# Weight and bias of the norms between stages applied by channel, behind the transposes

## The chip, the cores and the metric

The kernel runs on one core of a Trainium2 chip. The metric is the device time of one execution in microseconds (us). The core has five engines that work side by side, each in the order of its own queue: TensorE (PE; its weight loads are shown as PEld), VectorE (DVE), ScalarE (ACT), GpSimd (POOL) and SyncE (SP, which here issues DMAs). Each core has one SBUF and eight PSUM banks, in which matmuls and transposes leave their results.

## The reference

The program is one inference step of a two-layer encoder for 512 prompt frames and 8 x 16 sample frames, 640 tokens of 1024 channels in float32. There are six sub-layers: a feed-forward block, a mixer (a diagonal state-space part beside stick-breaking attention), a feed-forward block, and in the second layer a feed-forward block, a Mamba-2 mixer and a feed-forward block. Each one is wrapped in a norm:

```python
def layer_norm(x, g, b):
    xf = x.astype(jnp.float32)
    mu = jnp.mean(xf, axis=-1, keepdims=True)
    var = jnp.mean(jnp.square(xf - mu), axis=-1, keepdims=True)
    return ((xf - mu) * lax.rsqrt(var + LN_EPS) * g + b).astype(x.dtype)

def swiglu(x, w_gate, w_up, w_down):
    return (jax.nn.silu(x @ w_gate) * (x @ w_up)) @ w_down
```

A sub-layer computes x <- layer_norm(ALPHA * x + sublayer(x)); the feed-forward blocks count half. The result y of a norm is used twice: as the input of the next sub-layer, and as the residual that is added to its output.

## The kernel before, in words

**Stages.** The six sub-layers run one after the other: ffn0, mix0, ffn1, ffn2, mix1, ffn3. Between them lie five boundaries, named B1 to B5 here, each with a norm. A sixth norm ends the program; the change leaves it as it is.

**Tiles.** The 640 tokens are five tiles of 128. The sum of residual and sub-layer is kept in `yacc` with tokens on partitions (128 x 5 x 1024). The products of a stage want channels on partitions: `xt["hi"]` and `xt["lo"]`, 8 blocks of 128 channels by 640 tokens. Each float32 operand is split into a high part in a rounded format (a CAST on ACT, L95) and the remainder (a subtraction on DVE, L96), and each product is three matmuls, high x high, low x high and high x low (`mm3`, L134).

**A boundary.** For each tile t, `tm_proj` does the last projection of the old stage: two halves of 512 channels, 12 matmuls each, and DVE adds each half to `yacc` (L209; at B2 and B5 other lines). Then `layer_norm` follows: bn_stats and bn_aggr on DVE (L168, L169), an add of epsilon (L170), the power -1/2 on POOL (L171), the product with the mean on DVE (`nm`, L174), the normalise pass on ACT, whole width (L175), then the multiplication by g and the addition of b along the row: the lower half's multiply on DVE (L177), the upper half's on POOL (L178), both adds on POOL (L180, L179). The fifth tile does this with two whole-width instructions on DVE (L182, L184). g and b lie in `g_bc`, broadcast to all partitions by two DMAs from POOL's queue (L158). Last come the transposes: four of 128 x 128 into each of two PSUM banks (L196), and each bank is split into `xt` by CAST and remainder.

**Order.** `layer_norm` only puts its transposes on the list `pend`. `run_pend` takes the oldest one out: after the third, fourth and fifth tile's projection for the first three tiles, so that tile t's transposes stand behind the projection of tile t + 2, and for the last two tiles between the products of the next stage. A product over tiles 0 and 1 (256 columns) needs only two tiles, and there are four such products; the pass over tiles 2 to 4 (384 columns) comes behind them and needs all. Projections, transposes and splits of a boundary share a ring of four PSUM banks; the next stage's products use the other four. Which bank a tile gets, the program's builder decides, and a bank is written again when its last reader is done. At B1, B3 and B4 the second tile's transposes take the two banks that the first tile's had; at B2 the first two tiles have banks of their own. The engines' queues are otherwise filled in the order in which a scheduler in the builder puts the instructions.

In the names below T0 to T4 are the transposes of the five tiles; `T1`, `T2` and `T4` with a number are SBUF buffers of the feed-forward stage that hold g and b.

Of the kernel before, what the change touches and what calls it, by code (L numbers as in the profile page):

```python
# [36 lines left out]
def kernel(ctx: ExitStack, tc: tile.TileContext, I, O, phases=PHASES):  # L37
# [36 lines left out]
    make_identity(nc, ident)  # L74
    mhalf = const.tile([128, 1], F32, name="mhalf")
# [80 lines left out]
    def load_gb(n, g_bc):  # L156
        for j in range(2):
            nc.gpsimd.dma_start(g_bc[j], bass.AP(tensor=I["ln_gb"].tensor, offset=I["ln_gb"].offset + (2 * n + j) * D,  # L158
                                                 ap=[[0, 128], [1, D]]))

    def layer_norm(t, g_bc, last):
# [10 lines left out]
        if t < NT - 1 and not last:  # L172
            nm = mv[:, 1:2]
            nc.vector.scalar_tensor_tensor(nm, mv[:, 0:1], -1.0, rs, op0=ALU.mult, op1=ALU.mult)  # L174
            nc.scalar.activation(y, y, AF.Identity, scale=rs, bias=nm)  # L175
            lo, hi = slice(0, 512), slice(512, 1024)
            nc.vector.tensor_tensor(y[:, lo], y[:, lo], g_bc[0][:, lo], op=ALU.mult)  # L177
            nc.gpsimd.tensor_tensor(y[:, hi], y[:, hi], g_bc[0][:, hi], op=ALU.mult)  # L178
            nc.gpsimd.tensor_tensor(y[:, lo], y[:, lo], g_bc[1][:, lo], op=ALU.add)  # L179
            nc.gpsimd.tensor_tensor(y[:, hi], y[:, hi], g_bc[1][:, hi], op=ALU.add)  # L180
        else:
            nc.vector.scalar_tensor_tensor(y, y, mv[:, 0:1], g_bc[0], op0=ALU.subtract, op1=ALU.mult)  # L182
            for c in [slice(0, 512), slice(512, 1024)] if last and t == NT - 1 else [slice(0, 1024)]:
                state["ln"] = nc.vector.scalar_tensor_tensor(y[:, c], y[:, c], rs, g_bc[1][:, c],  # L184
                                                             op0=ALU.mult, op1=ALU.add).ins
                if last:
                    nc.sync.dma_start(O["y"][t * 128:t * 128 + 128, c], y[:, c])
        if last:
            return
        xh, xl = xt["hi"], xt["lo"]  # L190

        def transposes():
            for j in range(2):
                pt = bank_b().rearrange("p (k c) -> p k c", c=128)
                for k in range(4):
                    nc.tensor.transpose(pt[:, k, :], y[:, (4 * j + k) * 128:(4 * j + k) * 128 + 128], ident)  # L196
                split(xh[:, 4 * j:4 * j + 4, t * 128:t * 128 + 128],
                      xl[:, 4 * j:4 * j + 4, t * 128:t * 128 + 128], pt)
# [13 lines left out]
    def ffn(i, ph, last, side=None):  # L212
# [4 lines left out]
        with ExitStack() as st:  # L217
# [46 lines left out]
            for h in range(2):  # L264
                o, L = HALVES[h]
                for f in fs:
                    pg, pu = (bank_a()[:, :L] for _ in range(2))
                    for p, u in ((pg, wg[f][0]), (pu, wg[f][1])):
                        mm3(p, [w_k(u, k) for k in range(KT)],
                            [(xh[:, k, o:o + L], xl[:, k, o:o + L]) for k in range(KT)])  # L270
                    s = row(f)[:, o:o + L]
# [3 lines left out]
                    run_pend()  # L275
# [1699 lines left out]
```

## Time and profile before

| | |
|---|---|
| median of 3 runs | 2573.09 us (2572.42 to 2573.87) |
| profiled execution | 2573.02 us |
| its span, first to last instruction | 2571.3 us |
| mean granted TensorE clock | 0.992 |
| the norm at B1: T0 to T4 | 441.18 to 466.87 us |
| PSUM banks per tile at a boundary | 2 |

A page of the profile gives each engine's busy time with its share of the span, the chain of work that ended last, and groups of equal instructions. A row of the timeline gives the start in us, the busy time in us (of all xN instructions of a row), the engine, the line and the operation with what it writes and reads, the shapes, and in brackets how long the engine had been idle and who ended that. A row of a group gives, behind the bar, the busy time in us and the mean of one in ns, then the idle time ahead of it. A row of the windows gives the stretch in us, its length, how long the engine was busy in it and with how many instructions, the granted TensorE clock, and the DMA's share and rate.

### The profile page before, as it was taken

Reading aid. Unit: us, or ns where it says so; the run is one execution under the profiler, and the core shown is the slowest. Engines: PE = TensorE matmul, PEld = TensorE weight load, DVE = VectorE, ACT = ScalarE, POOL = GpSimd, SP = SyncE. Lnnn points to the kernel's source line nnn. Section 1 sums busy time; section 2 is a strip of 40 time slices with the busy share of each in tenths; the row PEclk is TensorE's granted clock in tenths of the full one; section 3 lists DMA queues with packets and bytes.
Section 4 is the critical chain, followed back from the end, with each engine's and each line's share of the span. In section 5 each row is a group of like instructions: output and inputs, shape, how many; then the busy total and the mean of one; then the engine's idle time right before and its main releaser. Section 6 shows DMA issues by size and latency. Waiting matters only on the chain. (4 is left out here: it accounts for less than half of the span.)

```text
span 2571.3 us, 40672 instructions
## 1 busy us (share of the span) xinstructions
PE 2511.2 (98%) x15577; PEld 2297.1 (89%) x15577; DVE 2017.1 (78%) x3685; ACT 1225.1 (48%) x2329; POOL 287.3 (11%) x412
## 2 busy tenths in 40 slices
PE   8999999999899999999999999999999999999998
PEld 8999999878678999998999999889989878999997
DVE  7788877666768888887888887778686798876768
ACT  4443444336743555553455554566565443443332
POOL 0000002110030000003000002311111150000001
PEclk9999999999999999999999999999999999999999
DMA  5332334443311334443144434356564722443442
GB/s 183 107 97 86 107 115 153 150 159 101 96 53 55 107 96 110 119 126 105 53 111 114 116 106 132 114 184 193 159 203 141 238 72 80 161 150 110 143 138 95
DMA packets 174835, 317.44 MB, mean 123 GB/s; under 512 B 20480, under 2 KB 91776, under 8 KB 174128
## 3 DMA queue, kind: packets, MB, share of 16 engines
q1 hardware_dynamic: 164816, 293.83, 35.7%
q0 software_dynamic: 9824, 21.01, 4.0%
q8 instruction: 122, 2.00, 0.3%
q14 instruction: 73, 0.60, 0.1%
HBM read 259.56 MB, written 40.54 MB: 117 GB/s over the span
## 5 line engine op out<-in xcount | busy, mean ns | idle before, releaser
L96 DVE TENSOR_TENSOR w<-raw,w 128x512 fp32r<-128x512 f32 (+1 forms) x601 | 525.8, 899 | 84.7 <-ACT w L95 83.6
L95 ACT CAST w<-raw 128x512 fp32r<-128x512 f32 (+1 forms) x601 | 442.3, 776 | 289.7 <-PE bank L134 106.9
L356 PE MATMUL bank<-xhi,w 128*128 128x320 f32 x2432 | 540.0, 309 | 1.0 <-ACT mx L367 0.9
L134 PE MATMUL bank<-xhi,w 128*128 128x256 f32 (+2 forms) x2272 | 502.5, 313 | 14.5 <-ACT xhi L95 8.2
L134 PE MATMUL bank<-w,h 128*128 128x512 f32 x1872 | 435.1, 390 | 0.0
L356 PE MATMUL bank<-T,w 128*128 128x320 f32 x2736 | 426.3, 309 | 0.8 <-DVE s L393 0.4
L134 PEld LDWEIGHTS bank<-w,h 128*128 128x128 f32 x1872 | 349.2, 188 | 72.5 <-DVE h L96 1.0
L356 PEld LDWEIGHTS bank<-xhi,w 128*128 128x128 f32 x2432 | 407.4, 188 | 5.0 <-ACT mx L367 1.8
L356 PEld LDWEIGHTS bank<-T,w 128*128 128x128 f32 x2736 | 406.4, 188 | 2.8 <-DVE s L393 1.2
L134 PEld LDWEIGHTS bank<-xhi,w 128*128 128x128 f32 x2272 | 382.2, 190 | 26.1 <-ACT xhi L95 9.5
L356 PE MATMUL bank<-xlo,w 128*128 128x320 f32 x1216 | 375.1, 308 | 0.0
L134 PE MATMUL bank<-xlo,w 128*128 128x256 f32 (+2 forms) x1136 | 353.8, 312 | 5.8 <-DVE xlo L96 5.8
L356 PEld LDWEIGHTS bank<-xlo,w 128*128 128x128 f32 x1216 | 228.0, 188 | 0.3
L134 PEld LDWEIGHTS bank<-xlo,w 128*128 128x128 f32 x1136 | 215.9, 190 | 7.7 <-DVE xlo L96 7.0
L209 DVE SCALAR_TENSOR_TENSOR yacc<-bank,yacc 128x512 f32<-128x512 f32 x160 | 109.4, 687 | 77.8 <-PE bank L134 77.2
L367 ACT COPY mx<-bank 128x320 f32<-128x320 f32 x228 | 96.4, 423 | 142.2 <-PE bank L356 141.7
L96 DVE TENSOR_TENSOR w<-sw,w 128x1024 fp32r<-128x1024 f32 x76 | 93.0, 1224 | 52.9 <-ACT w L95 52.6
L95 ACT CAST w<-sw 128x1024 fp32r<-128x1024 f32 x76 | 79.8, 1051 | 99.0 <-DVE sw L335 97.9
L500 POOL DMA_DIRECT2D yacc<-ev x56 | 48.6, 904 | 651.2 <-ACT ev L499 591.2
L134 PE MATMUL bank<-w,og 128*128 128x512 f32 x432 | 104.9, 396 | 3.0 <-DVE og L1769 2.8
L134 PEld LDWEIGHTS bank<-w,og 128*128 128x128 f32 x432 | 79.6, 188 | 21.0 <-DVE og L1769 4.6
L395 ACT ACTIVATE s<-s 128x320 f32<-128x320 f32 x108 | 50.8, 471 | 84.0 <-DVE s L393 83.8
(428 smaller groups left out, 3467.0 us busy)
## 6 DMA issues: line engine op xcount, KB each, us to landing
raw<-in_w_gate_dram SPq DMA_DIRECT2D x88, 512.0 KB, 3.8
raw<-in_w_up_dram SPq DMA_DIRECT2D x88, 512.0 KB, 4.0
raw<-in_w_down_dram SPq DMA_DIRECT2D x88, 512.0 KB, 3.6
raw<-in_m_in_dram SPq DMA_DIRECT2D x52, 512.0 KB, 4.6
yacc<-ev POOLq DMA_DIRECT2D x56, 256.0 KB, 4.3
raw<-in_m_out_dram SPq DMA_DIRECT2D x24, 512.0 KB, 4.1
csb<-cs_d SPq DMA_DIRECT2D x20, 512.0 KB, 4.9
h<-in_ssd_h_dram SPq DMA_DIRECT2D x16, 512.0 KB, 6.1
```

Of the source, the lines that this page charges most:

```text
L95: nc.scalar.copy(hi, src)
L96: return nc.vector.tensor_tensor(lo, src, hi.bitcast(F32), op=ALU.subtract)
L134: state["pe"] = nc.tensor.matmul(ps, a, b, start=(k == 0), stop=(k == n - 1)).ins
L209: state["acc"] = nc.vector.scalar_tensor_tensor(ya, pb, scale, ya, op0=ALU.mult, op1=ALU.add).ins
L356: nc.tensor.matmul(ps, A[p][:, a, k * 128:k * 128 + 128], B[p][b][:, k, :], start=(first and n == 0), stop=(n == 11), skip_group_check=True)
L367: nc.scalar.copy(e[n], ps)
L395: state["silu"] = nc.scalar.activation(t, ps, AF.Silu).ins
L500: nc.gpsimd.dma_start(yacc[:, t, 512 * j:512 * j + 512], e, accum_op=ALU.add)
```

## The change

For the five norms between stages:

- Every tile gets `nm` (L187) and the normalise pass on ACT (L188). The multiply and add by row ahead of the transposes are gone, for the fifth tile too.
- The transposes read the normalised values. Behind the four transposes into a bank, ACT goes over the bank in four pieces of 128 x 128, with g as scale and b as bias by channel, which are partitions there (L200). Then come the CAST and the remainder, as before.
- The residual gets g and b on POOL behind that: four instructions of 128 x 512 a tile, two multiplies and two adds (L206). They overwrite what the transposes read, so they wait for them.
- g and b by channel lie in `gb_all`, a table of 128 x 96 that one DMA from SP's queue loads at the start, behind the loads of x.
- The broadcast g and b take other buffers (T2 and T4 in the feed-forward stage; at B5 four halves).
- The last two tiles' transposes move: T3 behind the first product of the next stage and T4 behind the third, where they stood behind the second and the fourth (in mix1 behind the first and the second).

```diff
@@ layer_norm
-        if t < NT - 1 and not last:
-            nm = mv[:, 1:2]
-            nc.vector.scalar_tensor_tensor(nm, mv[:, 0:1], -1.0, rs, op0=ALU.mult, op1=ALU.mult)
-            nc.scalar.activation(y, y, AF.Identity, scale=rs, bias=nm)
-            lo, hi = slice(0, 512), slice(512, 1024)
-            nc.vector.tensor_tensor(y[:, lo], y[:, lo], g_bc[0][:, lo], op=ALU.mult)
-            nc.gpsimd.tensor_tensor(y[:, hi], y[:, hi], g_bc[0][:, hi], op=ALU.mult)
-            nc.gpsimd.tensor_tensor(y[:, lo], y[:, lo], g_bc[1][:, lo], op=ALU.add)
-            nc.gpsimd.tensor_tensor(y[:, hi], y[:, hi], g_bc[1][:, hi], op=ALU.add)
-        else:
+        if last:
...
+        nm = mv[:, 1:2]
+        state["ln"] = nc.vector.scalar_tensor_tensor(nm, mv[:, 0:1], -1.0, rs, op0=ALU.mult, op1=ALU.mult).ins
+        nc.scalar.activation(y, y, AF.Identity, scale=rs, bias=nm)
         xh, xl = xt["hi"], xt["lo"]
+        gb_t = state["gb_t"]
 
         def transposes():
+
+            c = slice(t * 128, t * 128 + 128)
             for j in range(2):
                 pt = bank_b().rearrange("p (k c) -> p k c", c=128)
                 for k in range(4):
                     nc.tensor.transpose(pt[:, k, :], y[:, (4 * j + k) * 128:(4 * j + k) * 128 + 128], ident)
-                split(xh[:, 4 * j:4 * j + 4, t * 128:t * 128 + 128],
-                      xl[:, 4 * j:4 * j + 4, t * 128:t * 128 + 128], pt)
+                for k in range(4):
+                    nc.scalar.activation(pt[:, k, :], pt[:, k, :], AF.Identity, scale=gb_t[:, 0, 4 * j + k:4 * j + k + 1],
+                                         bias=gb_t[:, 1, 4 * j + k:4 * j + k + 1])
+                split(xh[:, 4 * j:4 * j + 4, c], xl[:, 4 * j:4 * j + 4, c], pt)
+            for op, g in ((ALU.mult, g_bc[0]), (ALU.add, g_bc[1])):
+                for j in range(2):
+                    yj = y[:, 512 * j:512 * j + 512]
+                    nc.gpsimd.tensor_tensor(yj, yj, g[j] if isinstance(g, list) else g[:, 512 * j:512 * j + 512], op=op)
@@ ffn
                         mm3(p, [w_k(u, k) for k in range(KT)],
                             [(xh[:, k, o:o + L], xl[:, k, o:o + L]) for k in range(KT)])
+                        if p is pg:
+                            run_pend()
...
-                    run_pend()
@@ mix0
                     u_tile(m, h)
-                    if m % 2:
+                    if m % 2 == 0:
                         run_pend()
@@ mix1
             xbc_half(0, 0, 0)
+            run_pend()
             xbc_half(0, 1, 0)
             dt_half(0)
+            run_pend()
             gate_half(0, 0, 0)
@@ the load of x
                 nc.sync.dma_start(yacc[:, t, :], I["x"][t * 128:t * 128 + 128, :])
+            nc.sync.dma_start(gb_all.rearrange("p n j k -> p (n j k)"), I["ln_t"])
```

Three places in the order of the instructions, all at B1 (B3 and B4 have the same ones). The first is POOL's queue, from the power of one tile on; `rs` is the power, T1 and T2 hold g and b. Before:

```order
L171 TENSOR_TENSOR rs_4338<-rs_4338,mhalf_80 128x1
L178 TENSOR_TENSOR yacc_84<-yacc_84,T1_4284 128x512
L180 TENSOR_TENSOR yacc_84<-yacc_84,T2_4285 128x512
L179 TENSOR_TENSOR yacc_84<-yacc_84,T2_4285 128x512
L171 TENSOR_TENSOR rs_4380<-rs_4380,mhalf_80 128x1
```

With the change (`rs_4416` is the third tile's, `rs_4480` the fourth's, `rs_4544` the fifth's; T2 holds g and T4 holds b):

```order
L178 TENSOR_TENSOR rs_4340<-rs_4340,mhalf_81 128x1
L178 TENSOR_TENSOR rs_4378<-rs_4378,mhalf_81 128x1
L206 TENSOR_TENSOR yacc_85<-yacc_85,T2_4286 128x512 x2
L206 TENSOR_TENSOR yacc_85<-yacc_85,T4_4287 128x512
L178 TENSOR_TENSOR rs_4416<-rs_4416,mhalf_81 128x1
L206 TENSOR_TENSOR yacc_85<-yacc_85,T4_4287 128x512
L206 TENSOR_TENSOR yacc_85<-yacc_85,T2_4286 128x512 x2
L206 TENSOR_TENSOR yacc_85<-yacc_85,T4_4287 128x512
L178 TENSOR_TENSOR rs_4480<-rs_4480,mhalf_81 128x1
```

Two powers now stand ahead of the first tile's residual, and the third tile's power stands behind three of its four pieces, the fourth tile's behind three of the second tile's. At B5 it is all four, and a power for the mixer's own norm (L1770) stands between.

The second place is ACT's queue at the first tile's banks. Before, the two casts follow the second normalise pass:

```order
L175 ACTIVATE yacc_84<-yacc_84,mv_4379,rs_4380 128x1024
L95 CAST xhi_82<-bank_4434 128x4x128
L95 CAST xhi_82<-bank_4441 128x4x128
L175 ACTIVATE yacc_84<-yacc_84,mv_4421,rs_4422 128x1024
L95 CAST xhi_82<-bank_4490 128x4x128
```

With the change:

```order
L188 ACTIVATE yacc_85<-yacc_85,mv_4377,rs_4378 128x1024
L200 ACTIVATE bank_4424<-bank_4424,gb_all_80 128x128 x2
L200 ACTIVATE bank_4435<-bank_4435,gb_all_80 128x128
L200 ACTIVATE bank_4424<-bank_4424,gb_all_80 128x128
L200 ACTIVATE bank_4435<-bank_4435,gb_all_80 128x128
L188 ACTIVATE yacc_85<-yacc_85,mv_4415,rs_4416 128x1024
L200 ACTIVATE bank_4424<-bank_4424,gb_all_80 128x128
L200 ACTIVATE bank_4435<-bank_4435,gb_all_80 128x128
L96 CAST xhi_83<-bank_4424 128x4x128
L200 ACTIVATE bank_4435<-bank_4435,gb_all_80 128x128
L96 CAST xhi_83<-bank_4435 128x4x128
```

The third tile's normalise pass, which takes `rs_4416` above, now stands between the fifth and the sixth of T0's eight scales, ahead of both of T0's casts.

The third place is PE at the second tile's transposes, with the engines that each row waits for. Before:

```order
L196 MATMUL bank_4490<-ident_75,yacc_84 128x128 [waits DVE_49,Pool_49]
L196 MATMUL bank_4490<-ident_75,yacc_84 128x128 x3
L196 MATMUL bank_4497<-ident_75,yacc_84 128x128 [waits DVE_49]
L196 MATMUL bank_4497<-ident_75,yacc_84 128x128 x3
L134 MATMUL bank_4504<-w_4258,h_3898 128x512 [waits DVE_49]
```

With the change:

```order
L198 MATMUL bank_4488<-ident_75,yacc_85 128x128 [waits DVE_49,Activation_49]
L198 MATMUL bank_4488<-ident_75,yacc_85 128x128 x3
L198 MATMUL bank_4499<-ident_75,yacc_85 128x128 [waits DVE_49]
L198 MATMUL bank_4499<-ident_75,yacc_85 128x128 x3
L135 MATMUL bank_4514<-w_4260,h_3900 128x512 [waits DVE_49]
```

The wait for POOL is gone and one for ACT has come. `bank_4499` is the PSUM bank that `bank_4424` was, so its wait for DVE is one for the remainder of the first tile's first half; `bank_4514`, the fifth tile's projection, is the bank that `bank_4435` was. Before, both banks of the second tile's transposes were those of the first tile's.

More of the change, by code (lines that the diff above doesn't have):

```diff
@@ L74 @@
     make_identity(nc, ident)
+    gb_all = const.tile([128, 6, 2, 8], F32, name="gb_all")
     mhalf = const.tile([128, 1], F32, name="mhalf")
@@ L156, in load_gb @@
     def load_gb(n, g_bc):
+        state["gb_t"] = gb_all[:, n]
         for j in range(2):
[L158 to L159 removed]
+            parts = g_bc[j] if isinstance(g_bc[j], list) else [g_bc[j]]
+            L = D // len(parts)
+            for k, part in enumerate(parts):
+                nc.gpsimd.dma_start(part, bass.AP(tensor=I["ln_gb"].tensor,
+                                                  offset=I["ln_gb"].offset + (2 * n + j) * D + k * L,
+                                                  ap=[[0, 128], [1, L]]))
     def layer_norm(t, g_bc, last):
@@ L523, in down @@
                     g_bc = [wk.tile([128, 2, 4, Q], F32, name=f"T{n}", bufs=1).rearrange("p a k c -> p (a k c)")[:, :D]
-                            for n in (1, 2)]
+                            for n in ((1, 2) if last else (2, 4))]
                     load_gb(norm, g_bc)
@@ L1814, in mixer1 @@
                 if c == 0:
-                    g_bc = [wk.tile([128, 2, 512], F32, name="h0", bufs=4).rearrange("p a b -> p (a b)")
-                            for _ in range(2)]
+                    g_bc = [[wk.tile([128, 512], F32, name=n, bufs=2) for _ in range(2)] for n in ("xd", "xe")]
                     load_gb(LN_OF[ph], g_bc)
```

10 lines of the change are left out of this document (3 added, 7 removed).

## The prediction

> **What bounds the kernel now.** I read the page's busy shares first, then its chain.
>
> ```profile
> PE 2511.2 (98%) x15577; PEld 2297.1 (89%) x15577; DVE 2017.1 (78%) x3685; ACT 1225.1 (48%) x2329; POOL 287.3 (11%) x412
> PE 14%; DVE 2%; DMA 0%; issue 0%; ACT 0%; POOLq 0%; DVEq 0%; ACTq 0%
> ```
>
> TensorE is busy 98% of the span and leads the chain, so the change is worth what it does to TensorE's gaps at the five boundaries, B1 to B5. ACT's 48% and POOL's 11% are averages over the whole program and say little about 35 us at a boundary. The gaps stand in the timeline of PE; first B1, from the first tile's transposes (T0) to the last (T4):
>
> ```profile
> 441.18 1.04 PE L196 MATMUL bank<-ident,yacc 128*128 128x128 f32 x8
> 447.54 1.03 PE L196 MATMUL bank<-ident,yacc 128*128 128x128 f32 x8
> 453.88 1.04 PE L196 MATMUL bank<-ident,yacc 128*128 128x128 f32 x8
> 454.67 0.48 PE L134 MATMUL bank<-xhi,w 128*128 128x256 f32 x2
> 460.28 1.09 PE L196 MATMUL bank<-ident,yacc 128*128 128x128 f32 x8
> 466.87 1.03 PE L196 MATMUL bank<-ident,yacc 128*128 128x128 f32 x8
> 468.14 1.14 PE L134 MATMUL bank<-xhi,w 128*128 128x384 f32 x5 [0.24 <-ACT xhi L95]
> 472.11 0.69 PE L134 MATMUL bank<-xlo,w 128*128 128x384 f32 x1 [2.83 <-DVE xlo L96]
> ```
>
> A block of transposes costs TensorE 0.79 (453.88 to 454.67), a tile's projection 447.54 - 441.18 - 0.79 = 5.57, and one product of the next stage over the first two tiles (460.28 - 454.67) / 2 = 2.8. Without a wait the pass over tiles 2 to 4, which needs T4's split, would begin 5 x 0.79 + 2 x 5.57 + 4 x 2.8 = 26.3 after T0. B1 loses 0.24 + 2.83 = 3.07. The gaps of B2 (first row), B3 (two), B4 (two) and B5 (the rest):
>
> ```profile
> 784.22 1.97 PE L134 MATMUL bank<-xhi,w 128*128 128x384 f32 x5 [4.73 <-ACT xhi L95]
> 1207.16 1.14 PE L134 MATMUL bank<-xhi,w 128*128 128x384 f32 x5 [0.24 <-ACT xhi L95]
> 1209.17 0.44 PE L134 MATMUL bank<-xlo,w 128*128 128x384 f32 x1 [0.87 <-DVE xlo L96]
> 1620.61 1.09 PE L196 MATMUL bank<-ident,yacc 128*128 128x128 f32 x8 [1.61 <-POOL yacc L179]
> 1626.17 1.07 PE L196 MATMUL bank<-ident,yacc 128*128 128x128 f32 x8 [1.64 <-DVE yacc L184]
> 2102.08 1.09 PE L196 MATMUL bank<-ident,yacc 128*128 128x128 f32 x8 [0.83 <-POOL yacc L179]
> 2113.78 0.98 PE L134 MATMUL bank<-w,og 128*128 128x512 f32 x3 [2.06 <-DVE og L1769]
> 2115.06 3.48 PE L134 MATMUL bank<-w,og 128*128 128x512 f32 x14 [0.31 <-DVE og L1769]
> 2135.32 1.14 PE L134 MATMUL bank<-xhi,w 128*128 128x384 f32 x5 [2.72 <-ACT xhi L95]
> 2138.54 0.69 PE L134 MATMUL bank<-xlo,w 128*128 128x384 f32 x1 [2.08 <-DVE xlo L96]
> ```
>
> B2 loses 4.73, B3 1.11, B4 3.25, B5 8.0. What follows a gap shows in windows of 4 us (instructions, then the granted clock):
>
> ```profile
> 472.00:476.00 4.00, 3.89 (x12) 0.50 1.03 409
> 784.00:788.00 4.00, 3.78 (x12) 0.50 0.00 0
> 788.00:792.00 4.00, 4.00 (x24) 0.95 0.00 0
> 1626.00:1630.00 4.00, 3.83 (x34) 1.00 0.29 77
> ```
>
> After 2.83 and 4.73 idle, 12 matmuls run where 24 do at 0.95: 2.0 lost, and 0.2 behind it, 2.2 in all. After 1.61 and 1.64 (B4) nothing is lost. So a gap's price jumps between 1.64 and 2.83. The Trainium skill (TensorE: Matmul & The Clock Gate, Part 1) puts that jump at an idle window of about 3.4 us. The trace differs, with half rate after 2.83. By the page the waits of about 4.5 below are slowed too and the sum is the same, but the short waits in mid-boundary could not be, and the contention rival below would come to 2606.
>
> **The change, part by part.** *Removed:* the multiply and add by channel ahead of the transposes. DVE's part (one half a tile, and all of the last tile) PE's projections hide; where it or POOL's was late, it is in the gaps above (B4's 1.61 and 1.64, B5's 0.83), and I count those gaps as gone. *The last two transposes* move ahead by one product each, 2.8, so that a product covers their split. *The new DMAs* (one table at the start, first used 440 us later; the broadcasts in other buffers, two halves each at B5) are hidden by that distance; uncovered they would cost one landing.
>
> *Added on POOL* is what decides. The residual's four pieces now wait until a tile has been transposed, and in POOL's order the power of the tile after next stands behind three of them (four at B5). POOL and ACT at B1 before:
>
> ```profile
> 441.97 1.81 POOL L178 TENSOR_TENSOR yacc<-yacc,T 128x512 f32<-128x512 f32 x1 [1.55 <-ACT yacc L175]
> 443.87 1.29 POOL L180 TENSOR_TENSOR yacc<-yacc,T 128x512 f32<-128x512 f32 x1
> 445.12 1.30 POOL L179 TENSOR_TENSOR yacc<-yacc,T 128x512 f32<-128x512 f32 x1
> 446.37 0.56 POOL L171 TENSOR_TENSOR rs<-rs,mhalf 128x1 f32<-128x1 f32 x1
> ```
>
> ```profile
> 441.82 1.08 ACT L95 CAST xhi<-bank 128x512 fp32r<-128x512 f32 x2
> 447.15 1.24 ACT L175 ACTIVATE yacc<-yacc,mv,rs 128x1024 f32<-128x1024 f32 x1 [4.26 <-DVE mv L174]
> 454.80 2.69 ACT L95 CAST w<-raw 128x512 fp32r<-128x512 f32 x5
> ```
>
> A piece is 1.30 (L178's 1.8 has a multiply of DVE beside it), power to ACT's normalise 446.37 to 447.15, 0.78, the first bank full 0.64 after T0. A cast is 0.54.
>
> *Added on ACT:* eight 128x128 instructions a tile with two pointers, in the bank. No row has this; the nearest:
>
> ```profile
> L1542 ACT ACTIVATE acc<-ext,cw 128x128 f32<-128x128 f32 x24 | 11.7, 488 | 0.0
> 1637.35 1.20 ACT L1542 ACTIVATE acc<-ext,cw 128x512 f32<-128x512 f32 x2
> 2091.79 0.97 ACT L1768 ACTIVATE og<-yb,chp 128x128 fp32r<-128x128 f32 x3
> L209 DVE SCALAR_TENSOR_TENSOR yacc<-bank,yacc 128x512 f32<-128x512 f32 x160 | 109.4, 687 | 77.8 <-PE bank L134 77.2
> L96 DVE TENSOR_TENSOR xlo<-bank,xhi 128x512 fp32r<-128x512 f32 x50 | 33.0, 664 | 3.4 <-ACT xhi L95 3.3
> L272 ACT ACT_TABLE_LOAD x3 | 3.8, 1283 | 0.1
> L754 ACT COPY g<-bank 128x256 f32<-128x256 f32 x4 | 1.5, 373 | 4.8 <-PE bank L134 4.6
> L1661 ACT COPY bk<-bank 128x128 f32<-128x128 f32 x20 | 5.3, 263 | 1.0 <-DVE cbm L1657 1.0
> ```
>
> L1542 has scale and bias by pointer, 0.49 by itself; L1768, one pointer, follows every 0.3 (three in 0.97, the last one whole). These are the bounds, since each of the new ones has two pointers, and L1661's 0.26, a copy without any, is too far off for more than a rival. I take 0.40: L1542's 0.49 less an overlap of 0.1 (its two forms together took 1.20, the longer one 0.825 by its own group's mean).
>
> B1, us after T0's start. POOL: 0.65 + 3 x 1.30 = 4.55, power, third tile's normalise on ACT 5.33 to 6.57. Two queues stand behind this one wait. On DVE, behind the small product that takes the power, stand the next projection's accumulation, a BN_STATS and T0's remainders xlo; the first two (L209's 0.69, and about as much) are done by 6.9. On ACT, behind the normalise, stand the last scales and the casts of T0: the first cast ends at 7.9, the second at 8.85, and DVE's remainders (0.65) at 8.55 and 9.5. Who waits for those is PE, for the banks: in the built program T1's second bank is T0's first, so T1's second half, due at 6.76, waits until 8.55 (1.8), and the fifth tile's projection, due at 8.95 and using T0's second bank, until 9.5 (0.55). Round again: T1's second bank is full at 9.0, two pieces to 11.6, fourth normalise 12.4 to 13.6, T1's casts 15.0 and 16.5, T2's second half waits 0.15. Mid-boundary: 2.5.
>
> From there ACT has no gap but one: two weight casts to 17.5, T2's eight to 20.7, cast 21.25, the fifth normalise (POOL's four pieces of T2 from 15.65, power) 21.65 to 22.9, cast 23.45, a weight cast 24.0, T3's eight 27.2, two casts 28.3, three weight casts 29.9, three of T4 31.1, three copies at about 0.33 32.1, two more 32.9, T4's first cast 33.45. TensorE is there at 26.3 + 2.5 = 28.8 and waits 4.65. Loss 7.15 against 3.07: **+4.1**; half rate follows in both.
>
> B2: T0 and T1 have banks of their own, so T1 does not wait. T1's pieces run from 7.0, the fourth power at 11.2, normalise 12.0 to 13.2, T1's first cast 14.5; the next stage's first product, due at 13.5, waits 1.0 for it and some 0.3 in its middle for the second. What held T4's cast before is this:
>
> ```profile
> 783.07 0.62 ACT L95 CAST w<-raw 128x512 fp32r<-128x512 f32 x1 [3.35 <-DMA raw<-in_w_up_dram]
> ```
>
> A weight cast ahead of it waited for a landing; in the new order that cast stands behind T4's. ACT's chain is late instead: the walk of B1 with a table load (1.28), a silu and a cast of h, each about a copy's length, for the three copies puts T4's first cast at 33.5, where TensorE is at 27.6: loss 7.2 against 4.73, **+2.5**. B3, banks as B1, the table loaded already: cast at 33.25, loss 2.5 + 4.45 = 6.95 against 1.11, and a half-rate stretch that was not there, 5.8 + 2.2 = **+8.0**. B4, banks as B1, one more weight cast ahead of T4 and one less ahead of T3: cast at 33.4, loss 2.5 + 4.6 = 7.1 against 3.25, and 2.2, **+6.1**. B5: T0 comes at 2101.25, 0.83 sooner. Four pieces, a power for og and the norm's power end at 2108.2, T0's remainders at 2110.9 and 2112.5; a product that takes T0's first bank waits for the first, 1.7. The waits for og are over by then. The next stage's first product loses 0.5, T4's first cast ends at 2137.9 where TensorE is at 2131.7: 1.7 + 0.5 + 6.2 = 8.4 against 8.0, **+0.4**; both end in half rate.
>
> Sum 4.1 + 2.5 + 8.0 + 6.1 + 0.4 = 21.1. Against the profiled execution (2573.0: span 2571.3 and 1.7 around it; the median of the runs is 2573.1) that is **2594**.
>
> Bounds: 26 of the scales lie on the walk, at 0.30 each 2.6 less a boundary (-13, 2581), at 0.49 2.3 more (+12). POOL's first piece at 1.8 as L178: 0.5 a turn, two turns, +5. The waits of 1.8 and 0.55 may fall on the dear side of the clock's jump: +2.2 at three boundaries, +6.6. All three high: 2617.
>
> **Rivals.** *The gaps go (faster).* If banks or POOL's order did not bind and ACT kept up, the 20.2 of gaps and three half-rate stretches (6.6) could go: 2546 at best, half of it 2560. For it: no transpose waits for a POOL product any more, and T4 gains 2.8. Against: ACT alone, from T2's scales on, has 4 us more work than TensorE's 26.3 leaves. It decides if T4's first cast comes under 27 us after T0, which needs scales below 0.2. Chance 0.06.
>
> *Nothing measurable.* Scales at 0.26 as the plain copy L1661 and no half rate at B3 and B4: 21 - 26 x 5 x 0.14 - 4.4, about -1.5, 2571.5, within the 0.2% (5 us) that a measurement of this kernel can tell. Chance 0.06.
>
> *Contention (slower still).* POOL now works 20 pieces a boundary rather than 12, beside DVE's weight splits, and both lengthen: pieces of 1.8 throughout, 5 on each walk, +2.5 a boundary, and half rate already at T1: 21 + 12 + 7, 2613. Decides from where T1's wait passes 2.8. Chance 0.14.
>
> **Numbers.** Forecast 0.74. Slower by over 0.2%: 0.74 + 0.14 = 0.88; within: 0.06; faster: 0.06. Range 2581 to 2614: the bounds of the scales below, the contention case above.
>
> **What would show it.** Right: at B1, B3, B4 the second half of T1's transposes waits about 1.8 for DVE's xlo, POOL's powers (now L178) start behind three pieces, ACT is without a gap for 15 us up to T4's casts, and PEclk falls to 0.5 at all five boundaries. Wrong: no wait at T1, scales of a mean under 0.35 with a cadence of 0.2, or T4's cast ahead of the fourth product's end.

## The result, and the profile after

The changed kernel takes 2606.13 us (median of 4 runs, 2604.38 to 2607.74), the kernel before, run beside it, 2572.76 us (4 runs, 2570.48 to 2573.87). The ratio is 1.0126, interval [1.0112, 1.014]: 33 us slower.

From the profiled execution (span 2606.0 us), the page's busy shares and the head of its chain:

```profile
PE 2520.6 (97%) x15577; PEld 2303.5 (88%) x15577; DVE 2017.5 (77%) x3660; ACT 1299.7 (50%) x2534; POOL 327.0 (13%) x454
PE 78%; DVE 9%; ACT 6%; issue 2%; DMA 2%; POOL 2%; SPq 0%; POOLq 0%; DVEq 0%; ACTq 0%
```

TensorE runs the same 15577 matmuls. It is busy 9.4 us longer than before (2520.6 against 2511.2), at a mean granted clock of 0.989 instead of 0.992, and idle 85.4 instead of 60.1 (each span less the busy time), 25.3 more. The chain now has POOL in it with 2% of the span; that of before covers only a sixth of its span, so the two are not compared share by share. Where TensorE idles, its timeline shows. B1 from T0 on (first seven rows), B2 (one row), B3 (three), B4 (two), B5 (two):

```profile
442.35 1.04 PE L198 MATMUL bank<-ident,yacc 128*128 128x128 f32 x8
449.40 0.63 PE L198 MATMUL bank<-ident,yacc 128*128 128x128 f32 x4 [0.56 <-DVE yacc L217]
451.89 0.66 PE L198 MATMUL bank<-ident,yacc 128*128 128x128 f32 x4 [1.86 <-DVE xlo L97]
452.84 5.75 PE L135 MATMUL bank<-w,h 128*128 128x512 f32 x24 [0.29 <-DVE xlo L97]
460.19 0.66 PE L198 MATMUL bank<-ident,yacc 128*128 128x128 f32 x4 [1.16 <-DVE xlo L97]
469.76 1.04 PE L198 MATMUL bank<-ident,yacc 128*128 128x128 f32 x8
478.84 1.65 PE L135 MATMUL bank<-xhi,w 128*128 128x384 f32 x4 [5.30 <-ACT xhi L96]
773.51 0.50 PE L135 MATMUL bank<-xhi,w 128*128 128x256 f32 x2 [2.79 <-ACT xhi L96]
1197.50 0.66 PE L198 MATMUL bank<-ident,yacc 128*128 128x128 f32 x4 [1.86 <-DVE xlo L97]
1198.44 7.35 PE L135 MATMUL bank<-w,h 128*128 128x512 f32 x24 [0.29 <-DVE xlo L97]
1226.29 1.97 PE L135 MATMUL bank<-xhi,w 128*128 128x384 f32 x5 [6.14 <-ACT xhi L96]
1631.89 1.06 PE L198 MATMUL bank<-ident,yacc 128*128 128x128 f32 x4 [1.87 <-DVE xlo L97]
1659.84 1.65 PE L135 MATMUL bank<-xhi,w 128*128 128x384 f32 x4 [4.87 <-ACT xhi L96]
2143.78 0.36 PE L1767 MATMUL bank<-ones,ext 128*128 128x2 f32 x2 [2.05 <-DVE xlo L97]
2172.06 1.97 PE L135 MATMUL bank<-xhi,w 128*128 128x384 f32 x5 [6.89 <-ACT xhi L96]
```

Two kinds of waits make up most of it: T1's second half for a bank (1.86, 1.86, 1.87), and the pass over tiles 2 to 4 for T4's cast (5.30, 6.14, 4.87, 6.89; B2's, not shown, 3.40). At B2 the first product waits for T1's cast (2.79), at B5 a product for the bank of T0 (2.05). The same matmul in both traces, followed through the program, gives what each boundary adds: B1 +5.2, B2 +3.5, B3 +11.9, B4 +10.7, B5 +2.0, together 33.3. The stages between them give or take at most 2.4 each, 0.3 in all, and the way up to B1 adds 1.2.

What feeds those waits is POOL's order at B1, here in POOL's timeline of the changed kernel, with the mean-by-power operation in DVE's timeline behind it:

```profile
443.08 3.79 POOL L206 TENSOR_TENSOR yacc<-yacc,T 128x512 f32<-128x512 f32 x3 [3.50 <-issue]
446.83 0.55 POOL L178 TENSOR_TENSOR rs<-rs,mhalf 128x1 f32<-128x1 f32 x1
447.35 1.29 POOL L206 TENSOR_TENSOR yacc<-yacc,T 128x512 f32<-128x512 f32 x1
465.59 0.55 POOL L178 TENSOR_TENSOR rs<-rs,mhalf 128x1 f32<-128x1 f32 x1
466.11 10.91 POOL L206 TENSOR_TENSOR yacc<-yacc,T 128x512 f32<-128x512 f32 x8
```

```profile
447.42 1.24 DVE L187 SCALAR_TENSOR_TENSOR mv<-mv,rs 128x1 f32<-128x1 f32 x1 [3.01 <-POOL rs L178]
455.71 1.24 DVE L187 SCALAR_TENSOR_TENSOR mv<-mv,rs 128x1 f32<-128x1 f32 x1 [1.17 <-POOL rs L178]
466.18 1.23 DVE L187 SCALAR_TENSOR_TENSOR mv<-mv,rs 128x1 f32<-128x1 f32 x1 [1.39 <-POOL rs L178]
474.22 4.15 DVE L97 TENSOR_TENSOR w<-raw,w 128x512 fp32r<-128x512 f32 x3
```

The power stands behind three residual pieces, as forecast. New is the row after it. A product of two 128 x 1 columns takes 1.24 us, and it ends at 448.66, when POOL's running piece ends (447.35 + 1.29 = 448.64). The weight splits too are long beside POOL's eight pieces: of the three in 4.15 the first two took 1.69 and 1.75, and the third, behind POOL's last piece (466.11 + 10.91 = 477.02), 0.88. Not every one is held: a split at 469.80 took 0.68 beside the same row of pieces.

The Trainium skill (GPSIMD Engine Reference, Specifications) says that POOL shares its SBUF interfaces with DVE and that DVE instructions with two SBUF inputs contend for them. Both held operations read two tensors from SBUF, so the trace agrees in these rows; the runs below test it by the operands.

The hold on the splits is not new. In the kernel before, two of them took 2.92 at B1 beside POOL's pieces at 454.97 and 456.86:

```profile
456.14 2.92 DVE L96 TENSOR_TENSOR w<-raw,w 128x512 fp32r<-128x512 f32 x2
```

ACT at B1, the fifth tile's normalise pass and one bank pair of scales in the timeline, and the scales' group:

```profile
461.67 2.91 ACT L200 ACTIVATE bank<-bank,gb_all 128x128 f32<-128x128 f32 x8
467.45 1.25 ACT L188 ACTIVATE yacc<-yacc,mv,rs 128x1024 f32<-128x1024 f32 x1 [2.36 <-DVE mv L187]
```

```profile
L200 ACT ACTIVATE bank<-bank,gb_all 128x128 f32<-128x128 f32 x200 | 76.5, 454 | 8.3 <-PE bank L198 7.8
```

ACT idles 2.36 ahead of the fifth normalise, so the chain there is led by POOL's turn and not by ACT's work.

### The profile page after: what moved, and what is told of

It reads as the page before. It is cut to its first block, busy times and chain, and to the rows that moved or that the text cites. A ratio compares the mean times of both kernels' runs of the same rounds, so it can differ in the third digit from the quotient of the medians.

```text
span 2606.0 us, 40900 instructions
## 1 busy us (share of the span) xinstructions
PE 2520.6 (97%) x15577; PEld 2303.5 (88%) x15577; DVE 2017.5 (77%) x3660; ACT 1299.7 (50%) x2534; POOL 327.0 (13%) x454
## 4 chain that ended last, share of the span: by engine, by line
PE 78%; DVE 9%; ACT 6%; issue 2%; DMA 2%; POOL 2%; SPq 0%; POOLq 0%; DVEq 0%; ACTq 0%
PE bank L135 34%; PE bank L365 30%; PE bank L497 6%; DVE w L97 2%; PE bank L1030 2%; POOL yacc L206 2%; ACT w L96 1%; ACT bank L200 1%; ACT yacc L188 1%; DVE mv L187 1%; PE bank L869 1%; ACT xhi L96 1%; ACT es L84 1%; PE bank L1737 1%; PE bank L1713 0%
## 5 line engine op out<-in xcount | busy, mean ns | idle before, releaser
L97 DVE TENSOR_TENSOR w<-raw,w 128x512 fp32r<-128x512 f32 (+1 forms) x601 | 532.0, 909 | 82.9 <-ACT w L96 81.6
```

Source lines behind the costliest of these rows:

```text
L97: return nc.vector.tensor_tensor(lo, src, hi.bitcast(F32), op=ALU.subtract)
```

## The experiments

The theory from these traces: the residual on POOL is the price, by the power's place behind the pieces and by the hold on DVE. Rivals: the banks that T1 shares with T0; ACT's scales; the new places of the last transposes.

| run | median us | ratio to before | interval |
|---|---|---|---|
| the change | 2606.13 | 1.0126 | 1.0112 to 1.014 |
| no residual | 2562.89 | 0.996 | 0.9945 to 0.9975 |
| powers first | 2607.31 | 1.0129 | 1.0109 to 1.0149 |
| mean-by-power with pointer | 2601.48 | 1.0116 | 1.01 to 1.0132 |
| new places alone | 2558.52 | 0.9947 | 0.9934 to 0.996 |
| residual on DVE | 2567.09 | 0.9983 | 0.9973 to 0.9993 |
| no scales | 2582.82 | 1.0042 | 1.0027 to 1.0057 |
| one-input pieces | 2599.84 | 1.0112 | 1.0093 to 1.0131 |
| powers first, one-input pieces | 2578.04 | 1.0022 | 1.0009 to 1.0036 |
| two tiles on the new way | 2579.01 | 1.0031 | 1.0019 to 1.0043 |
| one tile on the new way | 2563.45 | 0.9964 | 0.9949 to 0.9978 |
| places, bias add on DVE | 2559.59 | 0.9953 | 0.9938 to 0.9967 |
| places, weight and bias on DVE | 2548.28 | 0.991 | 0.9895 to 0.9925 |

**The residual left out.** The four POOL pieces a tile are gone; the next stage's residual lacks weight and bias.

```diff
-            for op, g in ((ALU.mult, g_bc[0]), (ALU.add, g_bc[1])):
-                for j in range(2):
-                    yj = y[:, 512 * j:512 * j + 512]
-                    nc.gpsimd.tensor_tensor(yj, yj, ..., op=op)
```

> The residual's multiply and add on POOL are left out, so the residual of the next stage lacks weight and bias; everything else is as in the change. Theory: as with the powers first, 2558 to 2570, since the pieces cost through their place and through what they hold up on DVE; a difference to the powers-first kernel of more than 4 us would be what POOL's work beside DVE's weight splits costs. Rival 1 (ACT's scales): 2590 or more.

2562.89 us, 43 below the changed kernel. At B1 one wait is left in PE's timeline:

```profile
470.40 1.14 PE L135 MATMUL bank<-xhi,w 128*128 128x384 f32 x5 [2.53 <-ACT xhi L96]
```

The pass waits 2.74, 2.79, 2.38 and 1.81 at the other boundaries. T1's bank is shared as before and costs nothing. So the residual carries more than the whole loss. With it gone, T4's cast behind ACT's scales still makes PE wait about 2.5 a boundary.

**Powers first.** The pieces are the same, but all five powers of a boundary stand ahead of them on POOL.

```diff
-            for op, g in ((ALU.mult, g_bc[0]), (ALU.add, g_bc[1])):
...
+            owed.append(residual)
+            if t >= 2:
+                with tc.issue_after(state["pow"]):
+                    while owed:
+                        owed.pop(0)()
```

> All five powers of a boundary stand ahead of every residual piece in POOL's queue; ACT's and PE's orders and the banks stay those of the change. Theory (the power behind three pieces, and DVE's small product held by the piece that follows the power, pace the boundary): the time from power to normalise falls from 1.86 to 0.8 us, the second half of T1's transposes no longer waits for xlo, T4's first cast comes 27 to 29 us after T0 instead of 36.5, and the time is 2560 to 2570, below before. Rival 1 (the eight scales a tile on ACT pace it): T4's cast stays later than 33 us after T0 and the time is 2590 or more. Rival 2 (the PSUM bank that T1 shares with T0): T1's wait of 1.9 us stays, 2595 or more.

2607.31 us: no gain at all, though the mid-boundary waits are gone, T1's on the shared bank among them. The time is that of the two rivals, but neither explains it: T1 does not wait, and the pass over tiles 2 to 4 begins 30 to 32 after T0 at B1 to B4. The loss has moved. Counted as above, B4 adds 17.8 here instead of 10.7; the other boundaries add less than in the changed kernel (B1 4.3, B3 5.5), and the stages behind B2 and B3 add 2.3 and 4.3, by what is open. POOL, DVE and PE at B4 (one row of each timeline), and the group of the weight splits:

```profile
1637.40 24.71 POOL L208 TENSOR_TENSOR yacc<-yacc,T 128x512 f32<-128x512 f32 x20
```

```profile
1644.99 17.68 DVE L97 TENSOR_TENSOR w<-raw,w 128x512 fp32r<-128x512 f32 x1
```

```profile
1666.18 0.69 PE L135 MATMUL bank<-xlo,w 128*128 128x384 f32 x1 [15.07 <-DVE xlo L97]
```

```profile
L97 DVE TENSOR_TENSOR w<-raw,w 128x512 fp32r<-128x512 f32 x384 | 289.8, 784 | 27.0 <-ACT w L96 26.7
```

With 20 pieces back to back, one split took 17.68 and ended at 1662.67, 0.56 behind POOL's last piece (1637.40 + 24.71 = 1662.11); three more followed it and were through at 1664.72. The remainder queued behind them on DVE keeps TensorE idle for 15.07. My expectation left that hold out. The bank rival falls here: shared bank, early power, no wait.

**The mean-by-power product with a pointer.** One operand (the power) is given as a per-partition scalar, so that only one tensor is read.

```diff
-nc.vector.scalar_tensor_tensor(nm, mv[:, 0:1], -1.0, rs, op0=ALU.mult, op1=ALU.mult)
+nc.vector.tensor_scalar(nm, mv[:, 0:1], rs, -1.0, op0=ALU.mult, op1=ALU.mult)
```

> The small product of mean and power on DVE takes the power as a pointer scalar instead of as a second tensor operand; all orders are those of the change. Theory (DVE's instruction with two tensor operands in SBUF is held until POOL's running piece ends): it takes 0.16 us instead of 1.24, each of three normalise passes a boundary comes 1.08 sooner, T4's first cast about 2 to 3 us sooner at each of five boundaries: 2592 to 2598. Rival (a pointer operand is held as well, or the 1.24 is off the path): unchanged, 2604 to 2608.

All 25 of them with their minimum, median and maximum in ns:

```profile
L187 DVE TENSOR_SCALAR mv<-mv,rs x25: 212/214/216, 434.3 to 2152.2; 128x1 f32<-128x1 f32 x25
```

In the changed kernel the same line ranges from 159 to 1242. This form is never held. But 2601.48 us lies between my two forecasts, only 4.7 below the changed kernel by the medians, and the two intervals overlap. At B1 T4's cast still keeps PE waiting 5.23: the fifth normalise comes 23.5 after T0 instead of 25.1, TensorE comes earlier too, and the fifth tile's statistics on DVE stand behind weight splits of 1.75, 1.81 and 1.18. That the hold ends with the pointer form is shown; that this is worth much by itself is not.

**The new places alone.** The norm of the kernel before, with T3 and T4 behind the first and third product.

```diff
+                        if p is pg:
+                            run_pend()
...
-                    run_pend()
```

> The norm of before; only the last two transposes stand behind the first and third product, as in the change. Theory (the place by itself is worth little, since the late stalls come from POOL and ACT): T4 is asked for 2.8 us sooner and so waits more for DVE's last multiply-add at B1 to B3, the pass behind it less: within 6 us of before, 2567 to 2579. Rival (the place carries part of the loss): 2580 or more.

2558.52 us, 14 faster than before and more than I expected. What is left at B1 in PE's timeline is POOL's last add ahead of T3:

```profile
457.84 1.09 PE L196 MATMUL bank<-ident,yacc 128*128 128x128 f32 x8 [2.60 <-POOL yacc L179]
```

So the new places gain 14 in the norm of before, and the changed kernel is 48 slower than they alone are. Whether the same 14 is still in the changed kernel is not shown.

**The residual on DVE.** Same place in the program, same pieces, other engine.

```diff
-                    nc.gpsimd.tensor_tensor(yj, yj, ..., op=op)
+                    nc.vector.tensor_tensor(yj, yj, ..., op=op)
```

> The changed kernel with one word changed: the four 512-wide pieces of the residual (weight, bias) stand on VectorE at the same place in the program, instead of POOL. VectorE gets 4 x about 0.69 us = 2.8 us a tile, 13.8 us a boundary. Theory (POOL's two-SBUF-tensor pieces hold VectorE's own two-SBUF-tensor operations and the powers behind them): the powers start at once, the mean-by-power operation takes 0.16 again, the w splits take 0.69 each again; what is left is the 2562.9 us of the kernel without a residual plus what 2.8 us of VectorE work a tile delays of the splits: 2565 to 2590. Rival (the work itself is the price, wherever it runs, because VectorE's evictions and splits are the bound at a boundary): 2600 or more.

2567.09 us, 39 below the changed kernel, with 2.8 us a tile more on DVE. All mean-by-power products take 159 to 162 ns, and the group of the weight splits stands at 692 ns a piece, against 736 in the changed kernel:

```profile
L187 DVE SCALAR_TENSOR_TENSOR mv<-mv,rs x25: 159/159/162, 430.9 to 2118.2; 128x1 f32<-128x1 f32 x25
L97 DVE TENSOR_TENSOR w<-raw,w 128x512 fp32r<-128x512 f32 x384 | 254.5, 692 | 41.7 <-ACT w L96 36.3 <-DMA raw<-in_m_v_dram 4.8
```

The work is not the price; its engine is. An engine that was 77% busy took it for 4 us over the kernel without a residual, from one at 13%.

**No scales.** The changed kernel without ACT's scale and bias in the bank; the next stage's input lacks both.

```diff
-                for k in range(4):
-                    nc.scalar.activation(pt[:, k, :], pt[:, k, :], AF.Identity, scale=..., bias=...)
```

> The changed kernel without ScalarE's scale and bias in the bank (left out: the weight and bias of the next stage's input); the residual stays on POOL. If the costs add up (placement -14, scales in the bank about +4, residual on POOL +43 to the 2572 of before), 2598 to 2606. If ScalarE's chain of scales behind the last transposes is a price of its own that the residual only hides, 2580 to 2595.

2582.82 us, the second forecast of the two. With the residual on POOL, the scales cost 23. Without them PE's waits for T4's cast are gone (none named xhi stands in its table of waits), but three others came, two rows of that table:

```profile
PE bank L135 <- ACT hf L279: 13.2, 3, 5.7
PE bank L198 <- DVE yacc L214: 7.4, 3, 2.5
```

The parts do not add up, so no part has one price.

**One-input pieces.** Each POOL piece reads y alone, times 1.0; the next stage's residual lacks weight and bias.

```diff
-                    nc.gpsimd.tensor_tensor(yj, yj, ..., op=op)
+                    nc.gpsimd.tensor_scalar(yj, yj, 1.0, None, op0=ALU.mult)
```

> The changed kernel with the residual's four POOL pieces a tile reading one SBUF tensor instead of two (y times 1.0; so the next stage's residual lacks weight and bias). Everything else, their number, place and order, stays. Theory (a POOL piece with two SBUF tensors and a VectorE operation with two SBUF tensors hold each other up): the mean-by-power operation takes 0.16 instead of 1.24, the w splits about 0.69 each; the pieces themselves get shorter if their second tensor is what they pay for, and only their length still delays the power: 2560 to 2580. Rival (any POOL piece at work holds VectorE, whatever it reads): the mean-by-power operation still ends with the running piece, and the time is 2590 or more if the piece keeps its 1.3 us.

The pieces get no shorter (1.51 in the mean here, 1.37 before, by the groups' means), but the hold is mostly gone. POOL's pieces, the splits and the mean-by-power products:

```profile
L206 POOL TENSOR_SCALAR yacc<-yacc 128x512 f32<-128x512 f32 x100 | 148.9, 1510 | 30.0 <-PE bank L198 25.5 <-ACT og L1774 1.8 <-ACT xhi L96 1.6
L97 DVE TENSOR_TENSOR w<-raw,w 128x512 fp32r<-128x512 f32 x384 | 256.6, 697 | 41.2 <-ACT w L96 40.5
L187 DVE SCALAR_TENSOR_TENSOR mv<-mv,rs x25: 159/564/571, 432.9 to 2147.4; 128x1 f32<-128x1 f32 x25
```

0.57 instead of 1.24, and splits at 0.697 instead of 0.736, beside pieces that are longer. So what POOL does matters, as well as what DVE reads. (The piece changed its instruction with its operands, TENSOR_SCALAR for TENSOR_TENSOR; the runs do not tell the two apart.) But the time, 2599.84 us, misses my 2560 to 2580, and its interval overlaps the changed kernel's: with the power still behind three pieces, ending the hold gains little. (The profiled execution was the fastest of its runs, 2591.7 us; I take durations from it and not the time.)

**Both cures.** The edits of both runs in one kernel, so the next stage's residual lacks weight and bias.

```diff
-                        nc.gpsimd.tensor_tensor(yj, yj, ..., op=op)
+                        nc.gpsimd.tensor_scalar(yj, yj, 1.0, None, op0=ALU.mult)   # in the queued residual()
```

> Both cures together: all five powers ahead of all residual pieces, and each piece reads one SBUF tensor (y times 1.0; the next stage's residual lacks weight and bias). The pieces keep their number and nearly their length (100 of about 1.5 us). Theory (the loss of the changed kernel has two sources on POOL, each enough alone to keep most of it: the power behind pieces, and two-input pieces that hold VectorE's w splits): with both gone the time comes near that of the kernel without a residual, 2562.9: 2560 to 2576, with w splits at 0.69 to 0.72 in the mean. Rival (POOL's pieces cost by a third way, for instance by what they do to the next stage's work on POOL): 2585 or more, with a wait on POOL ahead of PE in the next stage.

2578.04 us: 28 below the changed kernel, where either cure alone gained 6 or nothing. It is 2 above my range, and the largest wait is of the rival's kind. At B4 POOL still has its row of pieces, and the Mamba stage's own small copies on POOL stand behind them. A row each of POOL's, ACT's and PE's timeline:

```profile
1617.37 18.25 POOL L208 TENSOR_SCALAR yacc<-yacc 128x512 f32<-128x512 f32 x12
```

```profile
1650.87 0.74 ACT L1562 ACTIVATE ext<-acc 128x640 f32<-128x640 f32 x1 [12.29 <-POOL cvo L1551]
```

```profile
1661.32 0.42 PE L1623 MATMUL bank<-ident,h 32*128 32x32 f32 x2 [11.83 <-DVE h L1612]
```

ACT waits 12.29 for a copy of 0.2, what stands behind it on ACT is late, and TensorE waits 11.83. As an estimate, 2578.04 less that one wait is 2566, near the kernel without a residual. The changed kernel has no such wait at this place (its own is 0.74). B4 adds 14.0 here; B1 and B2 take off 2.0 and 0.9.

**Looking for a faster kernel.** First, the new way only for the last tiles, with the residual's pieces behind the last power, and the old way for the others, in the new places:

```diff
+        in_bank = t >= 3   # in the second run t >= 4
...
+            if in_bank:
+                with tc.issue_after(state["pow"]):
+                    ...
```

> New places of the transposes; tiles 0 to 2 normalised, weighted and biased as in the kernel before, ahead of their transposes; only tiles 3 and 4 get the weight and bias in the bank, and their residual from POOL in 8 pieces behind the last power. Theory: the last two tiles lose the weight and bias from their way to the bank (about 2 us of POOL and VectorE pieces a tile), pay 4 x 0.4 us of ScalarE a bank, and 8 pieces (about 10 us) of POOL stand beside the next stage's w splits instead of 20: 2545 to 2565, against 2558.5 for the new places alone. If the 8 pieces hold the w splits as the 20 did, 2565 to 2580.

> As the mixed kernel with two tiles, with the last tile alone on the new way: 4 pieces (about 5 us) of POOL behind the last power. Theory: the hold on VectorE is half of that with two tiles and ends before the next stage's splits; the last tile's way to its bank is shorter by the weight and bias: 2545 to 2562. By the rival that ScalarE's scales at the end of the boundary cost as much as they save: 2558 to 2566, no better than the new places alone.

2579.01 and 2563.45 us. Neither beats the new places alone. With two tiles TensorE waits for T4's cast five times, 23.6 in all, a row of its table of waits; the eight pieces hold splits beside them, as DVE's timeline at B1 shows (of these three one took 0.68, two 1.77):

```profile
PE bank L135 <- ACT xhi L96: 23.6, 5, 6.6
```

```profile
461.29 4.07 DVE L97 TENSOR_TENSOR w<-raw,w 128x512 fp32r<-128x512 f32 x3
```

Then, from the new places alone, work taken off POOL: for tiles 0 to 3 one add (in the first run the middle line alone), or all three pieces.

```diff
-            nc.gpsimd.tensor_tensor(y[:, hi], y[:, hi], g_bc[0][:, hi], op=ALU.mult)
-            nc.gpsimd.tensor_tensor(y[:, lo], y[:, lo], g_bc[1][:, lo], op=ALU.add)
-            nc.gpsimd.tensor_tensor(y[:, hi], y[:, hi], g_bc[1][:, hi], op=ALU.add)
+            nc.vector.tensor_tensor(y[:, hi], y[:, hi], g_bc[0][:, hi], op=ALU.mult)
+            nc.vector.tensor_tensor(y[:, lo], y[:, lo], g_bc[1][:, lo], op=ALU.add)
+            nc.vector.tensor_tensor(y[:, hi], y[:, hi], g_bc[1][:, hi], op=ALU.add)
```

> The new places alone, with the bias add of the lower half moved from POOL to VectorE (tiles 0 to 3). POOL's chain between normalising and transposes loses one piece of 1.3 to 1.7 us, VectorE gains 0.69 a tile. Where the transposes of tile 3 waited 2.60, 1.43, 1.64, 1.63 and 0.87 us for POOL's last add, they wait about 1.3 less: 2550 to 2558, against 2558.5 for the new places alone. If VectorE's queue is the next bound there (its add stands behind w splits that POOL holds), 2556 to 2565.

> The new places alone, with weight and bias of tiles 0 to 3 wholly on VectorE: four pieces of 0.69 = 2.8 us a tile instead of one piece there and three of 1.3 to 1.8 on POOL (4.4 to 5.2). POOL is left with the power. Theory: the way from normalising to the transposes gets 1.6 to 2.4 us shorter, nothing holds the w splits, and VectorE's 2.1 us more a tile is below what the holds cost it: 2545 to 2558. Rival (VectorE is the bound at the boundary, as evictions, statistics and splits stand in one queue there): 2560 to 2580.

One add moved gains nothing (2559.59 us): T3's wait at B1 now ends on DVE, whose accumulation stands behind a split of 1.77 that POOL's last piece held.

```profile
458.56 0.63 PE L196 MATMUL bank<-ident,yacc 128*128 128x128 f32 x4 [1.67 <-DVE yacc L209]
```

All of it moved gives 2548.28 us, ratio 0.991 [0.9895, 0.9925]: the fastest of all, 23 us under the kernel before that ran beside it (2571.05). The weight splits' mean is 691 ns there. Its page and the one wait left at B1:

```profile
PE 2505.3 (98%) x15577; PEld 2293.3 (90%) x15577; DVE 2036.9 (80%) x3745; ACT 1227.1 (48%) x2329; POOL 199.4 (8%) x352
```

```profile
458.04 1.17 PE L196 MATMUL bank<-ident,yacc 128*128 128x128 f32 x8 [0.73 <-DVE yacc L179]
```

## Why the prediction was right, and where its sizes were off

**The verdict and the place** were right: slower, at all five boundaries, through POOL's order, T1's wait and T4's cast. T1's second half was forecast at 1.8 and took 1.86, 1.86 and 1.87; the powers start behind three pieces; the clock falls to half behind the waits for T4. The stages between the boundaries add next to nothing (0.3 in all).

**The size** was too small, 33.3 measured against 21.1, by boundary:

| | B1 | B2 | B3 | B4 | B5 |
|---|---|---|---|---|---|
| forecast | +4.1 | +2.5 | +8.0 | +6.1 | +0.4 |
| measured | +5.2 | +3.5 | +11.9 | +10.7 | +2.0 |

Three terms were off. That the time still lies in the range is in part luck: of what I had built its upper half from, only the half rate behind T1 came, and the held product was in none of its bounds.

*From power to normalise* I took 0.78 from the kernel before. It measured 448.69 - 446.83 = 1.86, because the product between them is held until POOL's next piece ends. In the kernel before no piece followed the power at once, so no row of this product showed it, though the splits' rows did show the hold. Three turns at B1 make 3 x 1.08 = 3.2; the fifth normalise came 25.1 after T0 instead of 21.65 and T4's cast about 36.4 instead of 33.45. That also corrects the sign "ACT without a gap": ACT had a gap of 2.36 ahead of the fifth normalise and none of note for the 12 us behind it. It is not the bound up to there, POOL's turns are. The 3.2 are not a price, though: the pointer run took the hold away and gained 4.7 over all five boundaries.

*The clock in mid-boundary.* I let T1's waits cost no half rate and kept 6.6 for it among the bounds. At B3 and B4 it came: the projection behind T1 took 7.35 and 6.95 instead of B1's 5.75. At B2 a wait of 2.79 stands where I had 1.0. My price went by the length of a single wait, and that is the step that fails here. Windows of the changed kernel, two at each of B1, B3 and B4 (length, PE busy and instructions, granted clock, DMA):

```profile
447.58:450.99 3.41, 1.89 (x10) 1.00 0.00 0
450.99:454.40 3.41, 2.22 (x11) 1.00 0.00 0
1195.09:1198.50 3.41, 1.26 (x9) 1.00 0.00 0
1198.50:1201.91 3.41, 3.41 (x8) 0.50 0.00 0
1628.58:1631.99 3.41, 0.98 (x7) 1.00 0.00 0
1631.99:1635.41 3.42, 3.42 (x10) 0.50 0.00 0
```

In this trace a spell at half rate begins on a grid of 3.41 us and lasts one to three steps of it: the first spells of B3 and B4 begin 433.49 apart, 127 steps. B1's windows lie on the same grid, 220 steps ahead of B3's spell. At B1 the waits fall into two steps, with 1.52 and 1.19 idle (length less busy), and the clock stays. At B3 and B4 one step has 2.15 and 2.43 idle, and the next one runs at 0.50. In the whole trace every spell follows a step with more than 1.7 idle, and none follows one with less than 1.6; in the other runs the two mix between 1.6 and 2.0, so no sharp limit is shown.

*The weight splits beside POOL.* The contention rival had POOL's and DVE's pieces lengthen together and put its 2613 on longer pieces. The residual pieces grew little (1.37 in the mean against the 1.30 I took). The DVE splits stand at 736 ns, against 692 without a residual on POOL, but the kernel before had 720 already. The group before and with the change:

```profile
L96 DVE TENSOR_TENSOR w<-raw,w 128x512 fp32r<-128x512 f32 x384 | 265.6, 720 | 47.6 <-ACT w L95 47.0
L97 DVE TENSOR_TENSOR w<-raw,w 128x512 fp32r<-128x512 f32 x384 | 271.7, 736 | 43.9 <-ACT w L96 43.2
```

So the change adds 16 ns a split, 6 us over the program's 384, and 11 us of hold lay in the kernel before. It is the true part of that rival, which I priced at the wrong engine. How much of these 6 us TensorE waited for is not shown.

The three terms do not add up to the missing 12.2, and how they share it is open.

**The scales** were about right in size: eight in 2.91, so about 0.36 apart, against 0.40. But I had them as ACT's load in a chain that ACT leads. The runs show that they cost 23 beside the residual on POOL, and that without the residual the whole new way is only 4 slower than the new places alone.

**The rival "gaps go"** was half true. The places alone gain 14, by a way I had put into the sum only as part of T4's cover; the other half of the change hid it.

**What caused the loss** is then settled in part. Shown: POOL as the residual's engine costs 39 to 43 (the run on DVE, the run without). Shown: the hold depends on what both sides do (pointer form, one-input pieces); for DVE it is the operands, since the same two operations with one of them in PSUM were not held. Shown: two of its ways, the power behind pieces and held splits, stand in for each other, so that one cure gains little and both gain 28. A third, the next stage's own POOL work behind the pieces, made a wait of 11.83 in the run with both cures; the changed kernel has none of that size there. Not settled: how much of the 33 belongs to each way in the changed kernel itself, since the costs don't add.

## What to carry to other kernels

An engine at 11% is no free place for work if its instructions stop a busier engine's: look at which DVE instructions stand beside POOL's and whether both read two tensors from SBUF, and price the DVE ones by the end of POOL's piece or, as in the powers-first run, of its whole row. Look for held rows in the kernel before, too: here they stood in its trace. Ask of every piece put on POOL what small operation queues behind it, the next stage's too. When a cure gains nothing, try it together with the second one before it is dropped.

## What the runs showed of the hardware that I had not expected

- A DVE product of two 128 x 1 SBUF columns took 0.16 us beside an idle POOL, 1.24 beside POOL pieces with two SBUF inputs, ending with the piece, 0.57 beside pieces with one, and 0.21 always when one operand was a per-partition pointer. Subtractions with one operand in PSUM (xlo) kept their 0.69 beside POOL, and so did the additions of a bank to `yacc` (0.68).
- The hold can outlast one piece: in the powers-first run one split took 17.68 us beside POOL's row of 20 pieces. At the other boundaries of that run splits beside the same row took 1.72 to 1.79, and one at each 0.68 or 0.69. What tells the cases apart no run shows.
- The same three waits, 0.56, 1.86 and 0.29 within 4.0 us, left the clock at 1.00 at B1 and were followed by 0.50 at B3; where they lay on the grid of 3.41 us tells the two apart (1.52 idle in a step at the most, against 2.15). The Trainium skill (TensorE: Matmul & The Clock Gate, Part 1) speaks of an idle window of about 3.4 us; here half rate followed windows of that length that were idle for only 2.15 and 2.43.
- A POOL piece of 128 x 512 with one SBUF input and a constant was no faster than one with two inputs, 1.51 against 1.37 us.
